# Four feed-forward stages whose moving tiles stand at four different byte distances from the weights

## The chip, the cores and the metric

The kernel runs on one core of one Trainium2 chip. The metric is the device time of one execution in microseconds (us); lower is better. A core has a matrix engine (TensorE, "PE" in the rows, its weight loads "PEld"), three engines for elementwise work (VectorE "DVE", ScalarE "ACT", GpSimd "POOL") and a queue engine (SyncE "SP"). SBUF is the on-chip memory of 128 partitions from which the matrix engine reads both operands.

## The reference

Two layers, each a feed-forward half-step, a token mixer and a second feed-forward half-step, with a layer norm after each. Sequence 256, model width 1024, feed-forward width 2816, all in float32:

```python
def swiglu_half(x, w1, w3, w2):
    return 0.5 * ((jax.nn.silu(x @ w1) * (x @ w3)) @ w2)

for l in range(DEPTH):                       # DEPTH = 2
    x = layer_norm(ALPHA * x + swiglu_half(x, ffn1_w1[l], ffn1_w3[l], ffn1_w2[l]), ln1_g[l], ln1_b[l])
    h = x @ w_in[l]
    ...
    mix = jnp.concatenate([out_a, out_b, out_c], axis=-1) @ w_out[l]
    x = layer_norm(ALPHA * x + mix, ln2_g[l], ln2_b[l])
    x = layer_norm(ALPHA * x + swiglu_half(x, ffn2_w1[l], ffn2_w3[l], ffn2_w2[l]), ln3_g[l], ln3_b[l])
```

The mixer's three parts (spatial gating, gated DeltaNet, gated linear attention) are not touched by the change. The four feed-forward stages, counted in the order in which they run, are stage 1 (layer 1, first half-step), stage 2 (layer 1, second), stage 3 (layer 2, first), stage 4 (layer 2, second).

## The kernel before

**Units of weights.** All weights are packed into units of 128 x 1024 float32 values, which arrive by DMA into a ring of five raw buffers (`load`). Nearly all units are then split into two tiles of the 32-bit matmul type (`conv`): `wh`, a rounded copy made by ScalarE (line 199), and `wl`, the remainder made by VectorE (line 200). The activations are split the same way (`split`, lines 232 and 233). A product is three matmuls one behind the other (`mm3`, lines 227 to 229): `wh` with the high half of the moving tile, `wh` with its low half, `wl` with its high half. Every matmul loads 128 x 128 weights and moves 256 columns (1024 bytes of each partition) past them; while it runs, the weights of the next one are loaded.

**A feed-forward stage** (`ffn`) walks over 22 blocks of 128 hidden features. For each it runs a unit of w1 into the bank `h1` and a unit of w3 into `h3` (8 x 3 matmuls each); the `epilogue` makes silu(h1) * h3 and splits it into the tile `gs`, which holds four blocks, high and low halves; two blocks later (`LAG`) a unit of w2 takes that block of `gs` as its moving tile and adds to the four banks `y`. The order is the program's: unit after unit on the matrix engine, without a scheduler that would move them.

**The moving tiles.** In stage 1 they are `xN`, views of the two buffers `xH`/`xL`. In stages 2 to 4 the first four blocks run on the not yet normalized `xH`/`xL` with two more columns (258, a row of 1032 bytes, so that the row for each further k stands 8 bytes further modulo 256), and the other 18 on `x2`, a pair of buffers under the tags `zrm` and `mAC` (in the rows these matmuls read `x`). In stage 4 the w2 units are turned round: `gs` is the weights and `wh`/`wl` move, 512 columns each (lines 516 to 518).

**Where tiles stand.** A tile's pool and tag set its byte address in the partition. The moving buffers have `XS = T + 8` columns a row where 256 would do, and there are two small tiles named `pad`; with them the addresses come out so that in all 256-column products the moving address minus the weight address is 192 modulo 256. Weight tiles, raw buffers and the 128-column steps inside a unit are all equal to each other modulo 256. So at line 227, 228 and 229 the distance is 192 everywhere but in the 258-column units, where it is 192 + 8k for k = 0 to 7. In stage 4's turned units it is 64.

The first three units of the program run unsplit in plain float32 (line 308); the last stage's tail, the layer norms and the mixer stand as they are in both kernels.

Of the kernel before, what the change touches and what calls it, by code (L numbers as in the profile page):

```python
# [11 lines left out]
F32R = mybir.dt.float32r  # L12
# [9 lines left out]
P = 128  # L22
L = 2
T = 256
D = 1024
KD = 8
DFF = 2816
XS = T + 8
NORM = 4
NF = DFF // P  # L30
NU = 2 * 3 * NF + 27 + 8
NRAW = 5
# [91 lines left out]
def trunk(ctx: ExitStack, tc: tile.TileContext, xin, w_all, cin, pin, lin, gin, out, dbg=None, nlayers=L):  # L124
# [7 lines left out]
    mx = ctx.enter_context(tc.tile_pool(name="mx", bufs=1))  # L132
# [15 lines left out]
    def ybank(i, name):  # L148
        return psy.tile([P, 512], F32, tag=f"y{i}", name=name)
# [34 lines left out]
    def conv(upto):  # L184
# [10 lines left out]

        i = b % NU - 3 * NF
        w = 1024 // next((c for o, c in CUTS if 0 <= i < o), 1)
# [6 lines left out]
    def whole(b):  # L204
        i = b % NU - 3 * NF
        return b < FIRST or 0 <= i < len(SEQ) and SEQ[i] in WHOLE
# [5 lines left out]
    def done(b):  # L212
        for d in (WH, WL, raw):
            d.pop(b, None)
        while st["conv"] < nunits and (sum(not whole(u) for u in range(b + 1, st["conv"])) < LOOK):
            conv(st["conv"])

    def next_unit():
        b = st["unit"]
        st["unit"] += 1  # L220
        need(b)
        return b
# [8 lines left out]
    def split(h, lo, src):  # L231
        A.copy(h, src)  # L232
        V.tensor_sub(lo, src, h.bitcast(F32))  # L233


    x = one.tile([P, KD, T], F32, name="x")

    xsplit = [one.tile([P, KD * XS], F32R, name=n) for n in ("xH", "xL")]
    xH, xL = (t[:, :KD * (T + 2)].rearrange("p (k c) -> p k c", k=KD) for t in xsplit)
    xN = [t[:, :KD * T].rearrange("p (k c) -> p k c", k=KD) for t in xsplit]  # L240
    xop = {"raw": (xH, xL), "norm": xN}
# [72 lines left out]
    def unit_tile(h, b, raw_in):  # L314
        w = T + 2 if raw_in else T
        for k in range(KD):
            mm(h, b, k, w)
# [2 lines left out]


    sums = [None, None]

    def lnc(l, n):
        return lnp[:, l, n].rearrange("p (k c) -> p k c", c=2)
# [72 lines left out]
    def raw_silu(dst, p, tag="t1"):  # L398
        cc = wk.tile([P, 1], F32, tag="cc", name="cc")
        V.tensor_copy(cc, p[:, T + 1:T + 2])  # L400
        t = raw_t(p, tag)
        act(dst, t, AF.Silu, bias=cc)


    def ffn(ln=None, last=None):
# [1 line left out]

        y = None
        gq, hq = {}, {}
        gs = mx.tile([P, 2, 4, T], F32R, tag="KQ", name="gs")  # L410
        if last:
            xT = [mx.tile([P, D], F32, tag=t, name="xT") for t in ("kb", "kd")]

        if ln:

            x2 = [mx.tile([P, KD * XS], F32R, tag=t, name="x2")[:, :KD * T].rearrange("p (k c) -> p k c", k=KD)
                  for t in ("zrm", "mAC")]
            xop["norm"] = x2

        def epilogue(f):  # L420
            h1, h3 = hq.pop(f)
            s = wk.tile([P, T], F32, tag="s", name="s")
            g = wk.tile([P, T], F32, tag="g", name="g")
            if ln and f < NORM:
                raw_silu(s, h1)
# [9 lines left out]
        pst = early = None  # L435
        for f in range(NF + LAG):
            if f < NF:
                if ln and f == 2:
# [16 lines left out]
                else:  # L455
                    if early is None:
                        b = next_unit()
                        unit_tile(h1, b, ln and f < NORM)
                        done(b)
# [6 lines left out]
                    b = next_unit()  # L466
                    unit_tile(h3, b, ln and f < NORM)
                    done(b)
# [20 lines left out]
            if f >= LAG:  # L489
                if y is None:  # L490
                    y = [ybank(i, f"y_{i}") for i in range(4)]
                if last and f == NF + LAG - 10:
                    for i in range(2):
# [638 lines left out]
        return y  # L1132


    for k in range(KD):
        split(xN[0][:, k], xN[1][:, k], x[:, k])
    for b in range(LOOK):
        conv(b)
    for l in range(nlayers):
        if l:  # L1140
            load_pl(l)
        y = ffn((l - 1, 2, 4 * EPS) if l else None)
        ln_open(y, 2.0 * ALPHA, l, 0)
        y = mixer(l, 0, 4 * EPS)
# [3 lines left out]
        if l < nlayers - 1:  # L1148
            y = ffn((l, 1, EPS))
            ln_open(y, 2.0 * ALPHA, l, 2)  # L1150
            continue
        Gb = mx.tile([P, D], F32, tag="vb", name="Gb")
        Bb = mx.tile([P, D], F32, tag="XP", name="Bb")
        y, xT = ffn((l, 1, EPS), (Gb, Bb))
        if dbg:
            dbg(f"x2_{l}", x)
        table(LNEXP)
        ends = []
        for tt in range(2):
            bst = mx.tile([P, 2, 6], F32, tag=f"bst{tt}", name="bst")  # L1160
            mv = mx.tile([P, 4], F32, tag=f"mvr{tt}", name="mv")
            m, t, r, v = (mv[:, i:i + 1] for i in (0, 2, 3, 1))
# [132 lines left out]
```

## Time and profile before

| what | value |
|---|---|
| times of three runs | 1126.73, 1131.29, 1131.29 us (median 1131.29) |
| the profiled execution's own time | 1116.8 us |
| its span | 1115.0 us |
| matrix engine busy | 1062.1 us, 95% of the span, 9872 matmul records |
| VectorE, ScalarE, GpSimd busy | 753.7, 600.2, 95.2 us |
| mean granted clock of the matrix engine | 0.982 |

The profiled execution is 14.5 us shorter than the median of the three timed runs. In a row of the profile a matmul's own duration (some 280 ns) is longer than its share of the time, since matmuls are pipelined: about 2.4 of them are under way at once. What a matmul costs in a stream without gaps is the step from its start to the next start, here called the pace. It comes out of a window that holds nothing else: the window's length by the number of matmuls, less the 2.4 that reach in from ahead of it. Lines are those of the kernel before; "h", "y", "pk" and the like are banks that a matmul writes, and the first name behind the arrow is the moving tile, the second the weights.

### The profile page before, as it was taken

The numbers are of one execution on the slowest core, as the hardware profiler recorded it, in microseconds if no ns is written. First come the engines' busy times: TensorE is split into PE (matmuls) and PEld (weight loads), VectorE is DVE, ScalarE is ACT, GpSimd is POOL, SyncE is SP. The second block draws the span as 40 slices with busy tenths as digits, with TensorE's granted clock in tenths as the row PEclk, the third lists the DMA queues.
The fourth block names the chain that finished last, engine by engine and source line by source line (L and its number), as shares of the span: only waits on it lengthen the run. The fifth ranks groups of instructions, "written<-read, shape, count | busy, mean of one in ns | idle before, by whom it ended". The sixth has DMA issues, their size and how long they took to land. (4 is left out here: it accounts for less than half of the span.)

```text
span 1115.0 us, 23694 instructions
## 1 busy us (share of the span) xinstructions
PE 1062.1 (95%) x9872; PEld 1014.1 (91%) x9872; DVE 753.7 (68%) x1254; ACT 600.2 (54%) x1063; POOL 95.2 (9%) x70
## 2 busy tenths in 40 slices
PE   8999999799999899999989999998989998999996
PEld 7999999787879899999889999997878798999995
DVE  4655556898877965555796555578988679655555
ACT  4444446577666744444574444455775567444442
POOL 0100001301012200000220000013010112000000
PEclk9999999899999999999999999998998999999998
DMA  8855554442323475555436555544423333755541
GB/s 270 299 195 193 193 199 155 133 138 75 130 79 122 152 230 187 188 189 188 142 118 233 187 186 183 186 150 133 152 76 111 102 112 137 243 191 191 190 167 38
DMA packets 51515, 182.38 MB, mean 164 GB/s; under 512 B 5840, under 2 KB 7376, under 8 KB 51280
## 3 DMA queue, kind: packets, MB, share of 16 engines
q1 hardware_dynamic: 50544, 177.23, 47.2%
q10 hardware_dynamic: 864, 3.64, 0.9%
q8 instruction: 77, 1.26, 0.5%
q14 instruction: 30, 0.25, 0.1%
HBM read 179.81 MB, written 1.05 MB: 162 GB/s over the span
## 5 line engine op out<-in xcount | busy, mean ns | idle before, releaser
L200 DVE TENSOR_TENSOR wl<-raw,wh 128x1024 fp32r<-128x1024 f32 (+1 forms) x455 | 412.9, 924 | 242.3 <-ACT wh L199 242.0
L199 ACT CAST wh<-raw 128x1024 fp32r<-128x1024 f32 (+1 forms) x455 | 351.9, 799 | 370.5 <-issue 188.6
L227 PE MATMUL h<-x,wh 128*128 128x256 f32 x864 | 241.5, 280 | 0.0
L228 PE MATMUL h<-x,wh 128*128 128x256 f32 x864 | 241.5, 279 | 0.0
L229 PE MATMUL h<-x,wl 128*128 128x256 f32 x864 | 241.5, 279 | 0.0
L228 PEld LDWEIGHTS h<-x,wh 128*128 128x128 f32 x864 | 164.7, 191 | 0.8
L227 PEld LDWEIGHTS h<-x,wh 128*128 128x128 f32 x864 | 162.2, 188 | 0.7
L229 PEld LDWEIGHTS h<-x,wl 128*128 128x128 f32 x864 | 162.2, 188 | 0.0
L227 PE MATMUL y<-gs,wh 128*128 128x256 f32 x528 | 148.2, 281 | 7.2 <-ACT gs L232 7.2
L228 PE MATMUL y<-gs,wh 128*128 128x256 f32 x528 | 148.5, 281 | 0.0
L229 PE MATMUL y<-gs,wl 128*128 128x256 f32 x528 | 148.4, 281 | 0.0
L228 PE MATMUL h<-xL,wh 128*128 128x256 f32 (+1 forms) x472 | 131.9, 280 | 2.1 <-DVE xL L342 2.1
L227 PE MATMUL h<-xH,wh 128*128 128x256 f32 (+1 forms) x472 | 133.1, 282 | 0.8 <-ACT wh L199 0.7
L229 PE MATMUL h<-xH,wl 128*128 128x256 f32 (+1 forms) x472 | 132.6, 281 | 0.5 <-DVE wl L200 0.5
L227 PEld LDWEIGHTS y<-gs,wh 128*128 128x128 f32 x528 | 99.8, 189 | 7.6 <-ACT gs L232 7.6
L228 PEld LDWEIGHTS y<-gs,wh 128*128 128x128 f32 x528 | 101.5, 192 | 0.2 <-DVE gs L233 0.2
L229 PEld LDWEIGHTS y<-gs,wl 128*128 128x128 f32 x528 | 100.1, 190 | 0.0
L228 PEld LDWEIGHTS h<-xL,wh 128*128 128x128 f32 x472 | 89.5, 190 | 3.0 <-DVE xL L342 2.6
L227 PEld LDWEIGHTS h<-xH,wh 128*128 128x128 f32 x472 | 89.7, 190 | 1.8 <-ACT wh L199 1.2
L229 PEld LDWEIGHTS h<-xH,wl 128*128 128x128 f32 x472 | 89.6, 190 | 1.1 <-DVE wl L200 0.9
L430 DVE TENSOR_TENSOR g<-s,h 128x256 f32<-128x256 f32 x76 | 32.0, 421 | 50.3 <-PE h L229 42.9
L345 POOL TENSOR_TENSOR s<-x 128x512 f32<-128x512 f32 x5 | 6.9, 1389 | 529.0 <-DVE x L338 529.0
(361 smaller groups left out, 1956.8 us busy)
## 6 DMA issues: line engine op xcount, KB each, us to landing
raw<-w_all SPq DMA_DIRECT2D x331, 512.0 KB, 4.3
raw<-w_all SPq DMA_DIRECT2D x12, 128.0 KB, 4.3
pl<-pin ACTq DMA_DIRECT2D x2, 730.5 KB, 7.8
cst<-cin ACTq DMA_DIRECT2D x1, 1026.0 KB, 8.1
x<-xin SPq DMA_DIRECT2D x4, 256.0 KB, 4.4
out<-xT SPq DMA_DIRECT2D x4, 256.0 KB, 2.0
Gb<-gin ACTq DMA_DIRECT2D x1, 512.0 KB, 3.5
Bb<-gin ACTq DMA_DIRECT2D x1, 512.0 KB, 3.3
```

Source lines behind the costliest of these rows:

```text
L199: st["copy"] = A.copy(WH[b][:, o:o + w], raw[b][:, o:o + w])
L200: V.tensor_sub(WL[b][:, o:o + w], raw[b][:, o:o + w], WH[b][:, o:o + w].bitcast(F32))
L227: PE.matmul(o, lhsT=wh, rhs=mh, start=first, stop=False, **kw)
L228: PE.matmul(o, lhsT=wh, rhs=ml, start=False, stop=False, **kw)
L229: PE.matmul(o, lhsT=wl, rhs=mh, start=False, stop=last, **kw)
L345: G.tensor_tensor(s2, x[:, 0:2], xs, op=ALU.add)
L430: V.tensor_mul(g, s, h3[:, :T])
```

## The change

A table `PLACE` of four numbers, one for each stage in the order in which they run: +16, +32, -16 and -32 bytes. Each call of `ffn` takes the next one, turns it into a number of columns `o` (4, 8, 60, 56; taken modulo 64 columns, so that -16 becomes +240 bytes), and lays its view of the moving tiles `o` columns into their buffers. For stage 1, whose `xN` is made before the first call, a line ahead of the loops does the same. With the 192 of before that gives 208, 224, 176 and 160 bytes modulo 256 for the moving tiles of the four stages, and 96 for the turned products of stage 4.

```diff
+PLACE = (0x10, 0x20, -0x10, -0x20)
...
+    ffns = [0]
...
-        gs = mx.tile([P, 2, 4, T], F32R, tag="KQ", name="gs")
+        o = PLACE[ffns[0]] // 4 % 64
+        ffns[0] += 1
+        gs = mx.tile([P, KD * XS], F32R, tag="KQ", name="gs")[:, o:o + KD * T].rearrange("p (a b t) -> p a b t", a=2, b=4)
...
-            x2 = [mx.tile([P, KD * XS], F32R, tag=t, name="x2")[:, :KD * T].rearrange("p (k c) -> p k c", k=KD)
+            x2 = [mx.tile([P, KD * XS], F32R, tag=t, name="x2")[:, o:o + KD * T].rearrange("p (k c) -> p k c", k=KD)
...
+    xop["norm"] = x0 = [t[:, PLACE[0] // 4 % 64:][:, :KD * T].rearrange("p (k c) -> p k c", k=KD) for t in xsplit]
     for k in range(KD):
-        split(xN[0][:, k], xN[1][:, k], x[:, k])
+        split(x0[0][:, k], x0[1][:, k], x[:, k])
```

The buffer of `gs` grows from 8192 to 8448 bytes, and the tiles that stand behind it in its pool move up by 256 bytes, which leaves their distances modulo 256 as they were. The mixer goes back to `xN` at its old place, and the 258-column units read `xH` and `xL` where they did. No instruction is added, removed or moved on any engine, and none waits for another one than before; only addresses differ.

## Rows read from the trace of the kernel before

**Rows 1.** From the profile's page: the header, the busy time of each engine, and its granted clock in 40 slices of the span.

```profile
span 1115.0 us, 23694 instructions
PE 1062.1 (95%) x9872; PEld 1014.1 (91%) x9872; DVE 753.7 (68%) x1254; ACT 600.2 (54%) x1063; POOL 95.2 (9%) x70
PEclk9999999899999999999999999998998999999998
```

**Rows 2.** Who waited for whom on the matrix engine, the longest sums of the whole span (us in total, times, longest).

```profile
PE pg L666 <- DVE hm L571: 9.0, 2, 4.5
PE y L227 <- ACT gs L232: 7.2, 2, 4.1
PE h L308 <- DMA x<-xin: 5.1, 1, 5.1
PE y L516 <- ACT gs L232: 4.1, 1, 4.1
```

**Rows 3.** Windows of the matrix engine alone: start and end in us, length, busy us with the number of matmuls, granted clock, DMA share, GB/s. The four are the steady stretches of stages 1, 2, 3 and 4, in this order.

```profile
18.20:189.40 171.20, 171.20 (x1512) 1.00 0.64 215
389.00:549.90 160.90, 160.90 (x1369) 1.00 0.58 196
585.30:746.30 161.00, 161.00 (x1369) 1.00 0.57 195
953.00:1096.00 143.00, 143.00 (x1060) 1.00 0.55 183
```

**Rows 4.** The same view of two stretches of the mixers, the k and q units of the first and of the second layer: the same lines, tiles and addresses, distance 192 in both.

```profile
224.50:239.00 14.50, 14.50 (x126) 1.00 0.43 143
779.00:795.00 16.00, 16.00 (x144) 1.00 0.34 116
```

**Rows 5.** Groups of instructions on the matrix engine by line and shape over the whole span: line, operation, tiles, shape, count, busy us, mean ns of one.

```profile
L227 PE MATMUL h<-x,wh 128*128 128x256 f32 x864 | 241.5, 280 | 0.0
L227 PE MATMUL h<-xH,wh 128*128 128x256 f32 x328 | 90.7, 277 | 0.0
L227 PE MATMUL h<-xH,wh 128*128 128x258 f32 x144 | 42.3, 294 | 0.8 <-ACT wh L199 0.7
```

**Rows 6.** The timeline of the matrix engine in two 258-column units of the first mixer, the first matmul of each k alone (start us, duration us). From one row to the next are three matmuls at one distance: 192 at the first row, then 200, 208, 216, 224, 232, 240 and 248, and again from 192 at 206.39.

```profile
203.52 0.28 PE L227 MATMUL pm<-xH,wh 128*128 128x258 f32 x1
...
203.88 0.28 PE L227 MATMUL pm<-xH,wh 128*128 128x258 f32 x1
...
204.24 0.28 PE L227 MATMUL pm<-xH,wh 128*128 128x258 f32 x1
...
204.60 0.29 PE L227 MATMUL pm<-xH,wh 128*128 128x258 f32 x1
...
204.97 0.28 PE L227 MATMUL pm<-xH,wh 128*128 128x258 f32 x1
...
205.32 0.28 PE L227 MATMUL pm<-xH,wh 128*128 128x258 f32 x1
...
205.69 0.28 PE L227 MATMUL pm<-xH,wh 128*128 128x258 f32 x1
...
206.03 0.28 PE L227 MATMUL pm<-xH,wh 128*128 128x258 f32 x1
...
206.39 0.28 PE L227 MATMUL pr<-xH,wh 128*128 128x258 f32 x1
...
206.75 0.28 PE L227 MATMUL pr<-xH,wh 128*128 128x258 f32 x1
...
207.11 0.28 PE L227 MATMUL pr<-xH,wh 128*128 128x258 f32 x1
...
207.47 0.29 PE L227 MATMUL pr<-xH,wh 128*128 128x258 f32 x1
...
207.84 0.28 PE L227 MATMUL pr<-xH,wh 128*128 128x258 f32 x1
...
208.19 0.28 PE L227 MATMUL pr<-xH,wh 128*128 128x258 f32 x1
```

**Rows 7.** The timeline of the matrix engine in stage 4: the first matmul of the first five k of a w1 unit that follows turned matmuls, then, behind the rest of this unit and a w3 unit, the first of twelve turned matmuls (512 columns) and the first matmul behind them.

```profile
967.26 0.28 PE L227 MATMUL h<-x,wh 128*128 128x256 f32 x1
...
967.61 0.28 PE L227 MATMUL h<-x,wh 128*128 128x256 f32 x1
...
967.97 0.28 PE L227 MATMUL h<-x,wh 128*128 128x256 f32 x1
...
968.31 0.28 PE L227 MATMUL h<-x,wh 128*128 128x256 f32 x1
...
968.65 0.28 PE L227 MATMUL h<-x,wh 128*128 128x256 f32 x1
...
972.73 0.39 PE L516 MATMUL y<-wh,gs 128*128 128x512 f32 x1
...
975.48 0.28 PE L227 MATMUL h<-x,wh 128*128 128x256 f32 x1
```

**Rows 8.** Groups of the splitting of `gs` on ScalarE and VectorE by shape: count, busy us, mean ns of one, idle before and its releasers.

```profile
L232 ACT CAST gs<-g 128x256 fp32r<-128x256 f32 x88 | 35.4, 402 | 5.0 <-DVE g L430 2.9 <-DVE g L427 2.1
L233 DVE TENSOR_TENSOR gs<-g,gs 128x256 fp32r<-128x256 f32 x88 | 36.9, 419 | 1.1 <-ACT gs L232 1.0
```

## Prediction

> **What bounds the kernel now.** I read the page first: the matrix engine is busy for 1062.1 of 1115.0 us, 95% of the span, and every slice of its clock is at 0.8 or more [rows 1]. Then its waits: the longest sum is 9.0 us and the only ones in the feed-forward stages are for `gs`, 7.2 and 4.1 us [rows 2]. So the end is set by the matrix engine's stream, and a feed-forward stage lasts as long as its matmuls take one behind the other. What is left to look at is the pace, and it is not one number. Windows without a gap at granted clock 1.00 give 171.20 / (1512 - 2.4) = 113.4 ns a matmul in stage 1, 160.90 / (1369 - 2.4) = 117.7 in stage 2 and 161.00 / 1366.6 = 117.8 in stage 3 [rows 3]. The durations say the same: the 864 first matmuls of stages 2 to 4 have a mean of 280 ns, the 328 of stage 1 one of 277 [rows 5]. All of these stand at distance 192.
>
> Two paces at one distance could come from the tiles, so I looked for the same tiles twice. The k and q units of the two mixers run the same lines on `xN` at the same addresses; the first layer's go at 14.50 / (126 - 2.4) = 117.3 ns, the second layer's at 16.00 / (144 - 2.4) = 113.0 [rows 4]. So distance 192 carries both a quick pace, 113.3, and a slow one, 117.8, and a stream keeps the one it fell into (for 170 us in stage 1). Stage 4 shows the falling in: each time the turned matmuls end, the next unit's k steps take 0.35, 0.36, 0.34, 0.34 us for three matmuls, which is two slow steps and then the quick pace [rows 7]. I take it that the two read streams, weights and moving columns, lock to each other in time, and that a restart decides how.
>
> The three timed runs lie 10 to 14.5 us above the profiled execution. If stages 1 and 4 fall into the slow pace too, the sum is: stage 1, 1509.6 x (117.8 - 113.4) = 6.6 us; stage 4, 288 x 3 = 864 matmuls of 256 columns, of which about 4 in 24 are slow already, so 864 x 20/24 x 4.4 = 3.2; its 264 turned matmuls at 2.75 us for twelve, 229 ns [rows 7], which could go to 2 x 117.8 = 235.6: at most 264 x 6.5 = 1.7. That is 11.5, and 1128.3 us. The median of 1131.29 is 3 us above that, which the mixers' streams can hold. So I read the median as "nearly everything slow" and the profiled execution as a lucky one.
>
> **The change part by part.** No instruction is added or moved, so there is nothing to count but the pace of the matmuls whose moving tile is shifted: 1509.6 in stage 1, 1366.6 each in stages 2 and 3, and 864 in stage 4, together 5107 [rows 3, 5], and the 264 turned ones. One nanosecond of pace on all of them is 5.1 us.
>
> The trace shows other distances only where rows of 1032 bytes make them pass by: in the 258-column units, three matmuls at each of 192, 200 ... 248 [rows 6]. The steps of the two units are, in us for three matmuls: at 192, 0.36 and 0.36; 200, 0.36 and 0.36; 208, 0.36 and 0.36; 216, 0.37 and 0.37; 224, 0.35 and 0.35; 232, 0.37 (once); 240, 0.34 (once); 248, 0.36 (once). Two columns more cost 0.8 ns at 2.4 GHz by proportion (2 in 256 of a pace near 113), so these are 117 to 122.5 ns for 256 columns. 208, stage 1's new distance, is level with 192 within the rows' resolution of 3 ns; 224, stage 2's, is level or up to 3 ns better. Here none has time to settle: the quick pace came after six matmuls at one distance [rows 7], and each distance has three.
>
> For 176 and 160 there is no row. By the nearest ones the bounds are the best and the worst that the passing rows show, 240 with 0.34 (113.3 less 0.8, so 112.5 ns) and 216 with 0.37 (123.3 less 0.8, so 122.5); I take 117.8, since five of the eight distances that pass by (192, 200, 208, 224 and 248) lie at 0.35 to 0.36. The same bounds serve the turned matmuls' step from 64 to 96: at most 264 x 9 = 2.4 us either way.
>
> The rest I cost at nothing. The splits write to addresses 16 or 32 bytes off: 402 ns on ScalarE and 419 on VectorE for one `gs` half [rows 8], 88 each; they have two units of 24 matmuls (2 x 24 x 113 = 5.4 us) as cover, and were they twice as long, 0.8 us more, they would still be inside it. The 256 bytes by which later tiles move change no distance. With that cover gone a doubled pair would cost 0.8 us a block, 88 x 0.8 = 70 us, which nothing here suggests.
>
> Engine ports are where a rule stands against the change. The trace says that two streams at one distance run at 113.4 or 117.8 ns, so something other than the matmul's own columns sets the pace. The Trainium skill, "TensorE: Matmul & The Clock Gate", Part 2, step 1, says that the matrix engine has two independent SBUF read ports and that loading the next weights takes no read bandwidth from the running matmul; no distance could matter by that. Its section "Back-to-back issue gap" gives N/2.4 + 2.5, 109.2 ns for 256 columns; at that pace in all four stages the sum would be some 44 us lower, as an estimate, and no row here is below 113 in a settled stream.
>
> **The forecast.** All four new distances have the same two paces as 192, and timed runs fall mostly into the slow one, as I read them to do now. Then nothing is moved: the median's 1131.29, or by the sum above 1128.3. I say 1130, with 1124 to 1137 as this case's own range (one stage quicker, or one nanosecond more on all).
>
> **Rivals.**
> - *The distance has no effect at all.* The pace would be set by the restart alone, as the two mixers' unequal streams at equal addresses [rows 4] allow. Same time, same range; by the skill's rule on the ports this is what must come. Against it stands that the 258-column steps repeat by distance in both units (0.37 at 216 twice, 0.35 at 224 twice) [rows 6].
> - *Faster: some of the new distances leave only the quick pace, or make the restart fall into it more often.* Priced by stage at 4.4 ns: 6.6, 6.0, 6.0 and 3.2 us. Two of them give 1119, all four 1109. For it: the quick pace exists, is stable for 170 us, and stage 4's restart finds it [rows 3, 7]. Against: the shift does not remove the overlap of the two streams, and nothing at 208 or 224 was quicker than at 192.
> - *Slower: at one of the new distances the two streams meet at a worse moment and stay there.* The place is stages 3 and 4, whose distances 176 and 160 no row covers. At 216's price, 122.5 - 117.8 = 4.7 ns, stages 3 and 4 give 10.5 us and 1141; all four 24 us and 1154. It decides from 5.7 us on, 1.1 ns on all 5107 matmuls, or 2.5 on stages 3 and 4. For it: of eight distances that pass by, 216 and 232 are clearly above 192, and only 240 clearly below. Also lost then is the quick pace that 192 can fall into.
>
> Lines of SBUF bear on which distances are alike. The rows put 216 and 232, odd multiples of 8 bytes, above 208 and 224, multiples of 16. The Trainium skill, "SBUF — State Buffer", section "Specifications (TRN2)", says that SBUF has lines of 16 bytes and that each step to a new line costs; by that, shifts of 16 and 32 bytes are the harmless kind, and the slower rival would lose its price. 248, an odd multiple too, is not above 192 in the rows, so I leave that rival most of its chance.
>
> **How the numbers follow.** The forecast has 0.28 and the rival without effect 0.10; both end within 0.5% of before (5.7 us; that is about what a measurement of this kernel can tell from no change): 0.38. Faster has 0.28 and slower 0.34, since a loss has no floor and the gain ends at the quick pace. For 8 in 10 the range reaches from all four stages quick, 1109, to all four at 216's pace, 1154: beyond each end about 1 in 10 is left, for distances worse than any row and for a pace below 113.
>
> **What would show it.** In the changed kernel's trace, the windows of the four steady stretches: 113 or 118 ns in each means the same two paces, and then the time follows from how many are quick. A third number, 115 or 120 and more, in one stage alone means that its distance matters, and the order of 208, 224, 176 and 160 says which way. The mixers' streams at 192 must stay at 113 or 118. I am wrong if a stage sits at a pace that no row of before shows, or if all four are quick in every run.

## The result and the profile after

The changed kernel takes 1133.23 us (median of 18 runs, 1126.32 to 1141.82); the kernel before, run beside it, 1120.34 (median of 18, 1113.98 to 1134.30). The ratio is 1.013, with a 95% interval of 1.0104 to 1.0157: slower by 1.3%. The time lies in the predicted range, but the forecast was that nothing is moved, and the change cost some 13 us. The three runs of before that stand ahead of the prediction (median 1131.29) were among the six longest of the 18. Medians here and below are of all runs of a kernel, while ratios leave out the runs that fell into the chip's slower state, which shows a lower granted clock.

The page after has the same shape as before [rows 1]: the matrix engine is busy for 95% of the span, now 1124.5 us, and no new wait has come in. In the rows below, lines 229 to 231 are the old 227 to 229, and 521 is the old 516. From the page:

```profile
span 1124.5 us, 23694 instructions
PE 1070.6 (95%) x9872; PEld 1021.9 (91%) x9872; DVE 753.4 (67%) x1254; ACT 600.6 (53%) x1063; POOL 95.3 (8%) x70
```

Who waited for whom on the matrix engine, the feed-forward stages' waits for `gs` (as in [rows 2]):

```profile
PE y L229 <- ACT gs L234: 7.3, 2, 4.1
PE y L521 <- ACT gs L234: 4.1, 1, 4.1
```

The waits are 7.3 and 4.1 us, as before. So the time is in the pace. The windows of the matrix engine in the steady stretches of stages 1, 2 and 3 (start and end, length, busy us with the number of matmuls, granted clock, DMA share, GB/s):

```profile
17.00:192.00 175.00, 175.00 (x1502) 1.00 0.63 211
397.00:557.00 160.00, 160.00 (x1355) 1.00 0.58 193
592.00:754.00 162.00, 162.00 (x1360) 1.00 0.59 195
```

Less the 2.4 matmuls that reach in, that is 116.7 ns at distance 208, 118.3 at 224 and 119.3 at 176, against 113.4, 117.7 and 117.8 [rows 3]. Stage 4, from the timeline (start us, duration us): the first matmul of some k steps of a unit at 160, then the first of twelve turned matmuls at 96, and the next unit.

```profile
967.02 0.28 PE L229 MATMUL h<-x,wh 128*128 128x256 f32 x1
...
969.16 0.28 PE L229 MATMUL h<-x,wh 128*128 128x256 f32 x1
...
969.51 0.40 PE L521 MATMUL y<-wh,gs 128*128 128x512 f32 x1
...
972.31 0.28 PE L229 MATMUL h<-x,wh 128*128 128x256 f32 x1
...
972.66 0.28 PE L229 MATMUL h<-x,wh 128*128 128x256 f32 x1
...
973.02 0.28 PE L229 MATMUL h<-x,wh 128*128 128x256 f32 x1
...
973.38 0.28 PE L229 MATMUL h<-x,wh 128*128 128x256 f32 x1
...
973.73 0.28 PE L229 MATMUL h<-x,wh 128*128 128x256 f32 x1
```

Six k steps take 2.14 us, 118.9 ns a matmul. The twelve turned ones take 2.80 us, 233.3 each, where 2.75 stood before [rows 7]. The unit behind them stays at 0.35 to 0.36 us for three; before, it fell to 0.34 after two steps. Averaged over all starts of the stage, 160 runs at 118.7 ns, and before ran at 113.8.

In us against the first trace of before: stage 1, 1510 x 3.3 = 5.0; stage 2, 1366 x 0.6 = 0.8; stage 3, 1366 x 1.5 = 2.0; stage 4, 864 x 4.9 = 4.2 and 264 turned x 4.1 = 1.1. That is 13.1; the span grew by 9.5, since the mixers, at 192 in both, went from 165.8 and 168.0 to 168.3 and 163.7 us, 1.8 less, and the rest is in starts and ends.

### The profile page after: what moved, and what is told of

Its sections match the earlier page's. It is cut to its first block, busy times and chain, and to the rows that moved or that the text cites. A ratio compares the mean times of both kernels' runs of the same rounds, so it can differ in the third digit from the quotient of the medians.

```text
span 1124.5 us, 23694 instructions
## 1 busy us (share of the span) xinstructions
PE 1070.6 (95%) x9872; PEld 1021.9 (91%) x9872; DVE 753.4 (67%) x1254; ACT 600.6 (53%) x1063; POOL 95.3 (8%) x70
```

## The experiments

The theory to begin with was that each distance has a pace of its own (theory 1); its rival, that the pace belongs to the stage and to how it is entered (theory 2).

**One distance for all four stages.** `PLACE` is replaced by four equal numbers:

```diff
-PLACE = (0x10, 0x20, -0x10, -0x20)
+PLACE = (0x10, 0x10, 0x10, 0x10)      # e1; 0x20 in e2, -0x10 in e3, -0x20 in e4
```

e1, all at 208. 

> All four stages at 208. Theory 1 (each distance has a pace of its own, whatever the stage): every stage runs at the 116.7 ns that stage 1 shows at 208 in the changed kernel, so stages 2, 3 and 4 gain 1.6, 2.6 and 2.0 ns a matmul over the changed kernel, 2.2 + 3.5 + 1.7 us, and the time is about 1126 against its median of 1133. Theory 2 (the pace belongs to the stage and to how it is entered, the distance has no part): stage 1 at 116.7, stages 2, 3 and 4 stay at 118.3, 119.3 and 118.7 and the time at 1133.

e2, all at 224. 

> All four stages at 224. Theory 1: 118.3 ns in every stage, stage 1 loses 2.4 us against the changed kernel, stage 3 gains 1.3 and stage 4 0.3, time about 1134. Theory 2: paces by stage as in the changed kernel (116.7, 118.3, 119.3, 118.7), time 1133.

e3, all at 176. 

> All four stages at 176. Theory 1: 119.3 ns in every stage, 3.9, 1.3 and 0.5 us more in stages 1, 2 and 4 than in the changed kernel, time about 1139. Theory 2: paces by stage as in the changed kernel, time 1133.

e4, all at 160. 

> All four stages at 160. Theory 1: 118.7 ns in every stage, 3.0 and 0.5 us more in stages 1 and 2 and 0.8 less in stage 3 than in the changed kernel, time about 1136. Theory 2: paces by stage as in the changed kernel, time 1133.

Measured, median and ratio to before with its interval: e1 1138.40 us, 1.0216 (1.0171 to 1.0260); e2 1134.76, 1.0176 (1.0133 to 1.0220); e3 1136.20, 1.0170 (1.0121 to 1.0218); e4 1134.87, 1.0178 (1.0131 to 1.0226). Windows of stages 1, 2 and 3 of e1:

```profile
18.00:196.00 178.00, 178.00 (x1496) 1.00 0.63 206
401.00:558.00 157.00, 157.00 (x1348) 1.00 0.61 194
595.00:753.00 158.00, 158.00 (x1356) 1.00 0.60 196
```

At 208, stages 2 and 3 run at 157 / 1345.6 = 116.7 and 116.7 ns, which is what theory 1 wanted, and not at the 118.3 and 119.3 of the changed kernel. But stage 1 runs at 178 / 1493.6 = 119.2, where the changed kernel had 116.7 at the same distance. So 208 has two paces, as 192 has. The same windows of e4:

```profile
19.00:196.00 177.00, 177.00 (x1494) 1.00 0.63 206
401.00:560.00 159.00, 159.00 (x1358) 1.00 0.61 196
598.00:757.00 159.00, 159.00 (x1358) 1.00 0.60 194
```

160 has 118.7 (stage 1) and 117.3 (stages 2 and 3). In e2 all stages are at 118.3 to 118.4, in e3 all at 119.1 to 119.3. Both theories were half right and were put together: each distance has a small set of paces, and the way in which a stream starts picks one of them. e1's forecast of 1126 fell with the single pace.

**Before once more, and both operands moved.** e5 is the kernel before, unchanged. 

> The kernel before once more, as a second trace of it. Theory 1 in the form that the first four runs leave (each distance has its own few paces, and a restart picks one of them): every stage at 192 runs at 113.3 or at 117.8 ns and at nothing between, but not necessarily the same stages as in the first trace (1 and 4 quick, 2 and 3 slow); the time between 1110 and 1131 by how many are quick. Theory 2 (the pace belongs to the stage): again 1 and 4 quick, 2 and 3 slow.

e6 moves weights and moving tiles by 32 bytes alike:

```diff
-    xH, xL = (t[:, :KD * (T + 2)].rearrange("p (k c) -> p k c", k=KD) for t in xsplit)
-    xN = [t[:, :KD * T].rearrange("p (k c) -> p k c", k=KD) for t in xsplit]
+    xH, xL = (t[:, 8:8 + KD * (T + 2)].rearrange("p (k c) -> p k c", k=KD) for t in xsplit)
+    xN = [t[:, 8:8 + KD * T].rearrange("p (k c) -> p k c", k=KD) for t in xsplit]
...
-    one.tile([P, 32], F32, name="pad")
+    one.tile([P, 40], F32, name="pad")
```

> Weights and moving tiles both 32 bytes further, so every distance is 192 (64 in the turned products) as before, and every address differs by 32. Theory 1 (the distance counts): paces 113.3 and 117.8 alone, time as before, 1112 to 1131. Rival (the moving tiles' own address modulo 256 counts): 118.3 ns in all stages as for 224 in the run with all four at 224, time about 1135.

e5 gave 1121.52 us, ratio 1.0011 (0.9969 to 1.0052), and e6 1126.12, ratio 0.9989 (0.9942 to 1.0037). Windows of stages 1 and 2, of e5:

```profile
17.00:194.00 177.00, 177.00 (x1505) 1.00 0.63 209
394.00:553.00 159.00, 159.00 (x1353) 1.00 0.60 194
```

and of e6:

```profile
19.00:195.00 176.00, 176.00 (x1496) 1.00 0.62 207
396.00:556.00 160.00, 160.00 (x1361) 1.00 0.60 195
```

Stage 1 of e5 runs at 177 / 1502.6 = 117.8 ns, where the first trace of the very same program had 113.4 [rows 3]: theory 2 falls, the pace of stage 1 is drawn anew in each execution. e6 has 117.8 too, and none of 224's 118.3. Its stage 4 is as quick as that of before: a window of 96 us in it holds as many matmuls, where 224 gave 709 in 100 us. Of e6, then of before:

```profile
963.00:1059.00 96.00, 96.00 (x703) 1.00 0.62 204
949.00:1045.00 96.00, 96.00 (x703) 1.00 0.62 205
```

So the moving tiles' own address does not set the pace; what counts is their distance to something that moved with them in e6. That this is the weight tile is the plain reading, but not shown alone: by the order of the pools the wider pad moves the raw buffers and the work tiles by 32 bytes too.

**Other distances.** `PLACE` is (0x30, 0x40, -0x80, -0x40) in e7 and (-0x08, -0x04, 0x04, 0x08) in e8.

> Stages 1 to 4 at 240, 0, 64 and 128. Theory 1: each stage steady at one of a few paces of its distance. By the passing rows of the 258-column units, 240 is the best (0.34 us for three, so near 113 ns); 0, 64 and 128 have no row, and by theory 1 they may lie anywhere from 113 up. If only 192 holds 113.3, stage 1 is above 116 ns. Theory 2 (the distance has no part): 113.3 or 117.8 in all four.

> Stages 1 to 4 at 184, 188, 196 and 200, half and quarter of the smallest shift of the change. Theory 1: paces other than 113.3 and 117.8 already at 4 bytes from 192, if the distance counts to the byte; if it counts by 16-byte steps, 196 and 200 keep 113.3 and 117.8 while 184 and 188 run at 176's 119.3. Theory 2: 113.3 or 117.8 in all four.

e7 took 1133.92 us, ratio 1.0118 (1.0047 to 1.0188), e8 1140.63, ratio 1.0177 (1.0107 to 1.0248). Windows of stages 1 to 3 of e8, at 184, 188 and 196:

```profile
17.00:197.00 180.00, 180.00 (x1501) 1.00 0.62 205
397.00:558.00 161.00, 161.00 (x1355) 1.00 0.59 193
597.00:761.00 164.00, 164.00 (x1357) 1.00 0.58 190
```

They are 120.1, 119.0 and 121.1 ns: four bytes beside 192 neither of its paces is there, so the distance counts to 4 bytes. At 188 and 196 these are means, the units run at 118.6 to 119.8 and at 120.5 to 121.7. Stage 4's starts give 120.3 at 200. In e7, 240, 0 and 64 run at 117.2, 120.1 and 117.8, and 128, by the starts in stage 4, at 118.6 in most units and 120.0 in some, 119.0 in the mean. The expectation that 240 be near 113, read off the passing rows, missed by 4 ns. One limit: stages 1 to 3 of e7 and e8 were traced once and hold no restart, and without one 192 too was slow in stages 2 and 3 of every trace. So a quick pace that 184, 188, 196, 240, 0 or 64 may also hold is not excluded. At 208, 224, 176, 160, 128 and 200 stage 4 was traced, whose turned products restart the stream more than a dozen times, and 113.3 never came.

**Restarting the stream on purpose.** e9 is before with four matmuls put in ahead of a w1 unit early in stages 1 to 3; what they write is overwritten by the unit:

```diff
                         b = next_unit()
+                        if f in (6,) and not last:
+                            for _ in range(4):
+                                PE.matmul(h1, lhsT=gq[f - 3][0][:, :P], rhs=WH[b][:, :512], start=True, stop=True,
+                                          skip_group_check=True)
                         unit_tile(h1, b, ln and f < NORM)
```

> The kernel before, with four matmuls of 512 columns put in ahead of one w1 unit early in each of stages 1, 2 and 3 (block 6 of 22): gs as the weights, the unit's wh as the moving tile, into the bank that the unit then overwrites. They make the matmul stream restart as stage 4's turned products do. Theory (at 192 a restart picks 113.3 or 117.8, and this kind of restart picks 113.3): from there on stages 1, 2 and 3 run at 113.3; price 4 x 229 ns in each stage, gain 4.4 ns on some 1100 matmuls, 4.9 us, in each stage that was slow; time 1112 to 1116 with less spread than before's 1111 to 1134. Rival (the pace hangs on the stage's other traffic, not on the restart): paces as before, time 2.8 us above before.

e10 has `range(1)`. 

> The same with one such matmul instead of four. Theory: if any break in the stream is a restart, stages 1 to 3 can go over to 113.3 here too, though which pace is picked may differ from the four; rival: paces as before, time 0.7 us above before.

e11 has e9's lines in e1, so at 208. 

> All four stages at 208 with the same four matmuls in stages 1 to 3. Theory (each distance has its own few paces, and 113.3 is none of 208's): the restart leaves 116.7 or 119.2 in every stage and nothing below, time 1125 to 1140. Rival (a restart of this kind gives 113.3 at any distance): 113.3 from block 6 on, time about 1110.

e9 took 1113.93 us, ratio 0.9969 (0.9937 to 1.0001). Its windows of stage 1 ahead of and behind the four, and of stages 2 and 3 behind them:

```profile
20.00:50.00 30.00, 30.00 (x257) 1.00 0.84 296
56.00:190.00 134.00, 134.00 (x1184) 1.00 0.59 192
...
425.00:560.00 135.00, 135.00 (x1194) 1.00 0.60 193
617.00:752.00 135.00, 135.00 (x1194) 1.00 0.59 193
```

Stage 1 goes at 30 / 254.6 = 117.8 ns up to the four and at 134 / 1181.6 = 113.4 behind them; stages 2 and 3, slow in every trace of before, go at 113.3. The timeline of stage 2 shows the change at the place (L460 are the four, 229 ns or so each):

```profile
422.73 0.28 PE L227 MATMUL y<-gs,wh 128*128 128x256 f32 x1
...
423.08 0.28 PE L227 MATMUL y<-gs,wh 128*128 128x256 f32 x1
...
423.79 1.09 PE L460 MATMUL h<-wh,gs 128*128 128x512 f32 x4
424.72 0.28 PE L227 MATMUL h<-x,wh 128*128 128x256 f32 x1
...
425.08 0.28 PE L227 MATMUL h<-x,wh 128*128 128x256 f32 x1
...
425.42 0.28 PE L227 MATMUL h<-x,wh 128*128 128x256 f32 x1
```

From 0.35 us for three ahead of it to 0.36 and then 0.34 behind. The single one of e10 works the other way round; its windows of stage 1 ahead of and behind it:

```profile
19.00:50.00 31.00, 31.00 (x276) 1.00 0.81 290
60.00:194.00 134.00, 134.00 (x1140) 1.00 0.58 187
```

Stage 1 had started quick, 31 / 273.6 = 113.3, and is slow behind the single matmul, 134 / 1137.6 = 117.8. The time was 1123.97 us, ratio 1.0044 (0.9997 to 1.0091). In e11 (1132.26 us, ratio 1.0117, 1.0040 to 1.0195) stage 2 changes at the four, and only between 208's own paces, from 16 / 134.6 = 118.9 to 138 / 1182.6 = 116.7:

```profile
400.00:416.00 16.00, 16.00 (x137) 1.00 0.77 262
420.00:558.00 138.00, 138.00 (x1185) 1.00 0.58 187
```

Stage 3 changes at the four the other way, from 16 / 136.6 = 117.1 (116.7 by the starts) to 141 / 1182.6 = 119.2; ahead of the four, then behind them:

```profile
596.00:612.00 16.00, 16.00 (x139) 1.00 0.79 257
616.00:757.00 141.00, 141.00 (x1185) 1.00 0.56 184
```

Stage 1 stays at 119.2. So a restart picks, and 113.3 came at 208 neither behind the four nor in stage 4. At 208 the kind of restart alone does not say which pace it picks: the same four matmuls made stage 2 quicker and stage 3 slower.

**One part undone.** e12 is the changed kernel with stage 4 back at 192, `PLACE = (0x10, 0x20, -0x10, 0)`. 

> The changed kernel with stage 4 alone put back to 192 (turned products at 64). Theory: stage 4 goes from 118.7 back to 113.8 ns (864 matmuls, 4.2 us) and its turned products from 233 to 229 (264, 1.0 us), stages 1 to 3 keep 116.7, 118.3 and 119.3; time 5.2 us under the changed kernel's 1133, so 1128. Theory 2 (distance has no part): 1133.

1129.41 us, ratio 1.0101 (1.0033 to 1.0169). Stage 4 lasts 191.4 us from its first matmul to its last, as in the traces of before (191.4 to 191.6), where the changed kernel has 196.9: 5.5 us, where 5.2 were expected. Its stage 1 was at 119.2, so 208's draw was the worse one this time. The time alone would not tell: its interval covers the changed kernel's ratio.

**How before draws.** e13 and e14 are before again, e15 is the changed kernel again, and e16 is e9 with the four matmuls at block 4 instead of 6.

> The kernel before, a third trace. Stage 4 quick (its turned products restart it), stages 1 to 3 each at 113.3 or 117.8. If the 13 us of the change come from before's quick stages, a time near 1115 to 1121 goes with at least one quick stage among 1 to 3, one near 1128 with none; if none of the traces has a quick stage 2 or 3, at most 6 to 13 us of the change are paces.

> The kernel before, a fourth trace, with the same expectation as for the third: stage 4 quick, stages 1 to 3 each at 113.3 or 117.8, and the time by how many of them are quick.

> The changed kernel, a second trace. Theory: no stage at 113.3; stage 2 at 118.3, stage 3 at 119.3 again, stage 1 at 116.7 or 119.2 and stage 4 at 117.3 or 118.7, the paces that 208 and 160 have shown; time 1126 to 1142.

> The kernel before with the four restarting matmuls at block 4 instead of 6. Theory: stages 1 to 3 at 113.3 from block 4 on, another 0.6 us better in each than with block 6, so about 1112 and under before in all rounds; rival: at this place the restart picks 117.8 in some stage, time no better than with block 6 (1114) or before (1121).

Stage 1 of e13 and of e14:

```profile
19.00:189.00 170.00, 170.00 (x1502) 1.00 0.65 214
```

```profile
17.00:194.00 177.00, 177.00 (x1505) 1.00 0.63 208
```

113.4 in e13, whose profiled execution took 1114.55 us, and 117.8 in e14, with 1118.16. Over the four traces of before stage 1 is quick twice (the first and e13), stages 2 and 3 never, stage 4 always. e14 did not take the 1128 that was expected of a trace with stages 1 to 3 slow: its mixers were 6 us shorter than e5's, though all four stages have the same paces in both. The second mixer tells why; e5's, then e14's (the granted clock is the third number from the end):

```profile
752.00:925.00 173.00, 159.87 (x1896) 0.92 0.34 108
749.50:915.50 166.00, 153.65 (x1896) 0.97 0.34 112
```

The same 1896 matmuls take 7 us longer at a mean granted clock of 0.92 than at 0.97. So a good part of before's spread is no draw of paces: over the 70 runs of before that the ratios of the experiments use, 0.01 less of the whole run's mean granted clock goes with some 7 us more (correlation -0.68). The change itself is not a matter of the clock: the mean is 0.981 over these 70 runs and over the changed kernel's 18. e15 (1139.31 us, ratio 1.0165, 1.0104 to 1.0225) has 119.2 in stage 1, then 118.3, 119.3 and 118.7, as expected. e16 took 1114.86 us, ratio 0.9952 (0.9923 to 0.9981): stages 1 to 3 quick from block 4 on, and the one kernel here whose interval lies below 1. It missed the expected 1112, and is not clearly better than e9. In the traces of e9 and e16 the four stages are 10 and 9 us shorter than in the mean of before's four traces; the ratios show 3.5 and 5.4 us, and where the rest goes was not traced. Its windows of stages 1 to 3, 113.3 ns each:

```profile
39.00:190.00 151.00, 151.00 (x1335) 1.00 0.63 201
396.00:546.00 150.00, 150.00 (x1326) 1.00 0.62 200
590.00:740.00 150.00, 150.00 (x1326) 1.00 0.63 199
```

## Why the prediction was wrong

- **What bounds the kernel** held: the time went where the pace went, with no wait added.
- **Two paces at 192, kept by a stream and picked by a restart** held, and was shown by putting restarts in (e9, e10).
- **"All four new distances have the same two paces as 192" failed.** This is the step on which the forecast stood. Each of the four has its own paces: 116.7 and 119.2 at 208, 118.3 at 224, 119.3 at 176, 117.3 and 118.7 at 160, and 113.3 came at none of them, stage 4's restarts included. So stage 4 lost 4.9 ns a matmul and stage 1, in the first two traces, 3.3.
- **"I read the median as nearly everything slow" failed too.** Three runs were taken for the rule, and their time above the profiled one was put down to paces alone; e5 and e14, with the same paces, lie 10 us apart, 7 of them in one mixer at a lower granted clock. Beside the changed kernel before's median is 1120.34; stage 4 is quick in every one of its traces and stage 1 in half of them. So there was something to lose, and the forecast had counted none of it. That the time still lies in the predicted range is luck: the 1131.29 taken for before is 11 us too high, and the loss of 13 us brought the changed kernel up to it.
- **The passing rows** [rows 6] were read as if three matmuls told of a steady stream. For 208 and 224 (119.2 and 115.9 ns after the 0.8) they were within their 3 ns of the truth, and had I taken 208 at its word, not as "level with 192", stage 1 would have come out slower than the profiled 113.4. For 240 their 112.5 was almost 5 ns off. That 0.34 does not even repeat: in the second unit, two rows behind the last of [rows 6], the step at 240 is 0.36. And the prediction's "117 to 122.5" for all of them leaves out its own 112.5 and 115.9.

```profile
208.56 0.28 PE L227 MATMUL pr<-xH,wh 128*128 128x258 f32 x1
...
208.92 0.28 PE L227 MATMUL pr<-xH,wh 128*128 128x258 f32 x1
```

- **The slower rival** named the mechanism that decided ("lost then is the quick pace that 192 can fall into"), but looked for it in streams that meet at a worse moment, on stages 3 and 4 at 4.7 ns. Stage 3 lost 1.5 ns; for stage 4 the price was near (864 x 4.7 = 4.1 us), though its new pace of 118.7 is far from 216's 122.5 and what it lost is the quick pace. The terms that weigh are stage 4, which lost a quick pace it always had (4.2 + 1.1 us), and stage 1, which lost one it has half the time.
- **The sum as it should have been**, with before's means over four traces and the changed kernel's over two: stage 1 from 115.6 to 118.0, 3.6 us; stage 2, 0.8; stage 3, 2.0; stage 4, 5.3: 11.7 us, against 12.9 by the medians and 11.7 to 17.6 by the ratio's interval. What is left, up to 6 us, was not traced; the mixers' streams at 192 draw as well, and their granted clock differs from run to run.
- **"The harmless kind"** did not hold: all four shifts are multiples of 16 bytes, and the quick pace came at none of the four new distances.
- **The rival without effect** fell with e1 to e4 and e8. The Trainium skill, "TensorE: Matmul & The Clock Gate", Part 2, step 1, has the weight load take nothing from the running matmul; here a shift of the moving tile by 4 bytes against the weights costs 1.2 to 7.8 ns of a matmul's pace, so "no distance could matter", which the prediction drew from the page, does not hold here; the measurement decides.
- **The edits costed at nothing** (splits to shifted addresses, later tiles up by 256 bytes) added no wait: those for `gs` are 7.3 and 4.1 us, 7.2 and 4.1 before.

Why 192 holds a pace that the four distances of the change lack, and what in a restart does the picking, stays open: the runs show which paces there are and that they are picked, not how the reads get in each other's way, nor even that it is these two reads that do.

## What to carry to other kernels

When a kernel is bound by one engine's stream, measure the pace of that stream by stage, as window length by instruction count, and in several executions: one trace can show the lucky draw of a program that has two. Do not read paces off the time of a run: here the granted clock moved it as much. The distance between a matmul's moving tile and its weights, modulo 256, was worth up to 7% of the pace here (113.3 to 121.1 ns), and a distance found good should not be moved by a few bytes in the belief that neighbours are alike. Where a stream has a quick and a slow pace, a few inserted matmuls that restart it can be worth more than their price (0.9 us in each stage here for up to 6 by the pace, and 0.5% of the kernel's time in all), but which kind of restart lands well has to be measured.

## What was not expected of the hardware

Paces in ns of 256-column matmuls with their next weight load, at full granted clock, by distance modulo 256, from all traces here. 184, 188, 196, 240, 0 and 64 stand on one stage of one trace, without a restart; 128 and 200 on stage 4 of one trace.

| distance | paces seen |
|---|---|
| 192 | 113.3 and 117.8 |
| 208 | 116.7 and 119.2 |
| 160 | 117.3 and 118.7 |
| 240 | 117.2 |
| 64 | 117.8 |
| 224 | 118.3 |
| 128 | 118.6 and 120.0 |
| 188 | 118.6 to 119.8 by unit, mean 119.0 |
| 176 | 119.3 |
| 184, 0 | 120.1 |
| 200 | 120.3 |
| 196 | 120.5 to 121.7 by unit, mean 121.1 |

A stream keeps its pace for 170 us, and the DMA traffic does not set it: 113.3 stands at DMA shares of 0.81 (e10) and 0.63 (e16), 117.8 at 0.84 (e9) and 0.58 [rows 3]. The same program draws differently from one execution to the next. Four matmuls of 512 columns turned stages 1 to 3 to the quick pace at 192 in the one trace of each of the two kernels that had them; one such matmul turned a quick stage slow, in one trace.
